# A two-layer hybrid encoder on one core: the pooling branch's GpSimd sums take a later place behind the decay chain, and a small lower-bound computation moves behind the seventh weight chunk

## The chip, the cores and the metric

The kernel runs on one core of a Trainium2 chip. The metric is device time in microseconds (us) for one execution, as the median over runs. A core has five engines with queues of their own: PE (TensorE, matrix products; its weight loads are listed as PEld), DVE (VectorE), ACT (ScalarE), POOL (GpSimd) and SP (which here issues transfers). Each engine works its queue strictly in order; an instruction whose inputs or buffers are not ready holds up everything behind it on that engine.

## The reference

The input is x with 256 tokens of 1024 features in float32. Each of two layers computes

```
x = x + 1/2 * SwiGLU_1(RMSNorm(x))
z = RMSNorm(x) @ W_in      # pool 512 | q 512 | f 512 | i 512 | out-gate 512 | branch gates 2*1024
A = causal pooling of the pool columns: 4 groups, trailing windows 2/4/8/16,
    (window mean - value) @ pool_w[g], times pool_scale
B = HGRN2 gated linear recurrence: 4 heads, 128x128 state, forget gates bounded below by lb
x = x + W_out( sigmoid(g_A) * (A @ W_pa) + sigmoid(g_B) * (B @ W_pb) )
x = x + 1/2 * SwiGLU_2(RMSNorm(x))
```

and a last RMSNorm follows. The lower bounds lb come from a softmax and a running sum over the layers' `lb_logits`, 512 numbers per layer.

## The kernel before

Weights stream in chunks of 128x2048 float32 (`stream`, `chunk`). Each chunk is split on the chip into a rounded part `hi` (ACT, L128) and a remainder `lo` (DVE, L129), and PE multiplies with both (L186 and L188, L216 to L218). There are four buffers for raw chunks and three each for `hi` and `lo`.

`mixer` (L480) holds the part that the change touches. PE first makes the f, i and q columns; then twelve steps follow (the list `steps`): two for the pool columns (`pool_in`), two for the output gate (`out_gate`, sigmoid and L673), eight for the branch gates (`gate`, L680). Each of the last ten is 24 products of 128x128 by 128x512 in L216 to L218.

Between the steps the recurrence is worked off in eight pieces, the list `recur`: seven levels, n = 1, 2, 4, 8, 16, 32, 64, and `across`. Piece i is made in step i, and its products are made in step i + 1. A level (`level`) does this:

- DVE multiplies the keys with the decays `suf` (L554) and the queries with the decays `pre` (L555) into a tile `m` of which there are two buffers.
- POOL then lengthens the decays for the next level: `suf` by L556, and `pre` by L557. L557 overwrites what L556 reads, and the next level's L554, L555 and L556 read what these two write: L556 and L557 of all levels are one chain.
- PE makes eight products from `m` (L590) in one of two PSUM tiles `gps`, and DVE takes them into the score matrix (`keep`, L565; for n = 64 ACT, L597).

The pooling branch shares POOL with that chain. `pool_group(g)` makes the running sums of group g by doubling (L636, one to four additions of about 270 columns), corrects the first 16 columns by L640 and L642, and DVE finishes the rest (L643). `pool_product(g)` multiplies the result with `pool_w` on PE (L650, L651), in one of the same two `gps` tiles, and ACT and DVE write the two parts of the product (L654, L655). All four are needed when the products with `W_pa` begin, after the twelfth step. `outputs()` (L693 on) forms the branch's output in step 9, also through `gps` tiles.

The order on each engine is laid out when the program is built: a planner with a model of durations takes, whenever an engine is free in its model, the ready instruction that stands first in the program; what is traced inside `urgent()` counts as standing 300 places earlier. The pieces of the recurrence are inside `urgent()`; the pooling calls are not. `tc.issue_after(x)` adds one rule: instructions traced in the block on x's engine are queued behind x there. Instructions of other engines in the block are not bound by it.

`lower_bounds()` (L311) runs once, in the first layer: three tiny DVE instructions (L314, L316), two exponentials on ACT (L317), and eight more tiny DVE instructions. Its result is read in the first mixer.

Of the kernel before, what the change touches and what calls it, by code (L numbers as in the profile page):

```python
# [10 lines left out]
F32 = mybir.dt.float32  # L11
# [3 lines left out]
ALU = mybir.AluOpType  # L15
# [10 lines left out]
NH = 4  # L26
# [42 lines left out]
def _body(ctx, tc, a, out):  # L69
    nc = tc.nc  # L70
# [9 lines left out]
    tt = nc.vector.tensor_tensor  # L80
# [35 lines left out]
    at = [0]  # L116
# [10 lines left out]
    def parts(raw, hi, lo, sl):  # L127
        a = nc.scalar.copy(out=hi[:, sl], in_=raw[:, sl])  # L128
        return a, tt(out=lo[:, sl], in0=raw[:, sl], in1=hi[:, sl].bitcast(F32), op=ALU.subtract)  # L129
# [14 lines left out]
    def prepare_first():  # L144


        chunks = [chunk() for _ in range(FIRST)]
        for j0, j1 in PIECES:
            sl = slice(j0 * CH // KD, j1 * CH // KD)
            c0 = 0 if j0 == 0 else NVEC + j0 * S  # L150
            xsl = slice(c0, NVEC + j1 * S)
            x = (nc.scalar if j0 == 1 else nc.sync).dma_start(out=xg[:, xsl], in_=a["x"][:, xsl])
            if j0 == 1:
                with tc.issue_after(x.ins):
                    nc.scalar.activation(table, table, AF.Silu)
            for i, (src, _, raw, hi, lo) in enumerate(chunks):
                (nc.scalar if i == j0 == 0 else nc.sync).dma_start(out=raw[:, sl], in_=src[:, sl])
                last = parts(raw, hi, lo, sl)
                if i == 0:
                    for j in range(j0, j1):  # L160
                        scaled(j, C_F1, j > 0)
        return last

    def weights(key, ahead=3):
        i = next(n for n, s in enumerate(stream) if s[0] == key)
# [79 lines left out]
    def split(out, src):  # L245

        nc.scalar.copy(out=out[0], in_=src)  # L247
        tt(out=out[1], in0=src, in1=out[0].bitcast(F32), op=ALU.subtract)  # L248

    def scaled(j, gain, first=False):  # L250

# [137 lines left out]
    def ffn(l, f, sq, gain):  # L389
        hs = slots(range(11), F32R)  # L390

        def hidden(k):
            return hs[k // 2].rearrange("p (k two) s -> p k two s", two=2)[:, k % 2]

        def gate_up(ms):
            if done:

                with tc.issue_after(done.pop().ins):
                    ws = [weights((f, l, "gu", m)) for m in ms]
            else:  # L400
                ws = [weights((f, l, "gu", m)) for m in ms]
            pss = [[pmm.tile([P, 2, S], F32, tag="mm", name="ps") for _ in range(2)] for _ in ms]
            if len(ms) == 1 and ((l, f) != (0, 0) or ms[0] > 5):

                for ks in ((range(6), range(6, KD)) if ms[0] == 0 else (range(KD),)):
                    order = [(k, g) for k in ks for g in range(2)]
                    wide_run(ws[0], [(pss[0][g], (k * 2 + g) * P, xs(k), k == 0, k == KD - 1) for k, g in order])
                return list(zip(ms, pss))
            for k0, k1 in PIECES:
                for w, ps in zip(ws, pss):  # L410
                    for kk in range(k0, k1):
                        for g in range(2):
                            c = (kk * 2 + g) * P
                            mm_wide(ps[g], w, slice(c, c + P), xs(kk), kk == 0, kk == KD - 1)
            return list(zip(ms, pss))

        def evacuate(m, pss):
            if m < 2:
                with urgent():
                    z = pair_sum(pss)  # L420
            else:
                z = pair_sum(pss)
            tt(out=z, in0=z, in1=bc(rb, 2), op=ALU.mult)  # L423
            s = tmp.tile([P, S], F32, tag="s", name="s")
            gate = nc.scalar.activation(s, z[:, 0], AF.Silu)
            h = tmp.tile([P, S], F32, tag="h", name="h")
            tt(out=h, in0=s, in1=z[:, 1], op=ALU.mult)  # L427
            split([hidden(m)[:, 0], hidden(m)[:, 1]], h)
            return gate

        n = FIRST if (l, f) == (0, 0) else 1
        groups = [range(n)] + [[m] for m in range(n, KF)]
        wait = gate_up(groups[0])
        if sq is None:
            sq = Squares()
            for j in range(KD):
                add = sq.add(j)
                if j == 1:

                    with tc.issue_after(add.ins):  # L440
                        nc.gpsimd.dma_start(out=cst, in_=a["cst"])
        with urgent():
            rc = norm_columns(sq)
        rb = None
        for ms in groups[1:]:
            wait += gate_up(ms)
            if rb is None:
                rb = norm_row(rc)
            for m, ps in wait:
                gate = evacuate(m, ps)  # L450
            wait = []
            if (f, m) == (0, 6):
                poolw = act.tile([P, NH, P], F32, tag="poolw", name="poolw")
                nc.sync.dma_start(out=poolw, in_=a["pw"][:, l])
                pw.append(poolw)
            if (l, f, m) == (0, 0, 6):
                with tc.issue_after(gate.ins), tc.issue_after(latest[1].ins):
                    lower_bounds()
                nc.sync.dma_start(out=tab, in_=a["tab"])
            if gain is None and m == 6:  # L460
                fin.extend(t.rearrange("p a b -> p (a b)") for t in slots((11, 12, 13)))
                nc.sync.dma_start(out=fin[0], in_=a["fin"])
            if gain is None and 8 <= m < 12:
                by_token(m - 8)
        if gain is None:
            return last(hidden)
        sq = Squares()
        for j in range(KD):
            ps = pmm.tile([P, 2, S], F32, tag="mm", name="ps")
            for h in range(2):  # L470
                w = weights((f, l, "dn", j, h))
                kks = [(k, h * (KF // 2) + k) for k in range(KF // 2)]
                wide_run(w, [(ps, k * P, hidden(kk), kk == 0, kk == KF - 1) for k, kk in kks])
            with urgent():
                nc.vector.scalar_tensor_tensor(
                    out=xT[:, j], in0=ps[:, 1], scalar=0.5, in1=xT[:, j], op0=ALU.mult, op1=ALU.add)
            residual(j, ps[:, 0], 0.5, gain, sq)
        return sq

    def mixer(l, sq, gain):  # L480
        big = [P, NH, S]
        kk_, pre, suf, og4 = slots((0, 2, 3, 4))
        kk_, pre, suf = (t.rearrange("p (b h) (u t) -> p b (h u) t", b=2, u=2) for t in (kk_, pre, suf))
# [54 lines left out]
        def at(t, n, first, second, one=False):  # L538


            part, (sb, _), *_ = t.ap
            return bass.AP(t.tensor, t.offset + first, [
                part, (sb + second - first, 2), (2 * n, NH * P // (2 * n)), (0 if one else 1, n)])
# [4 lines left out]
        def later(t, n):  # L548
            return at(t, n, n, 0)

        def decayed(n, left, right):

            sl, pr = earlier(suf, n), later(pre, n)
            tt(out=left, in0=earlier(kk_, n), in1=sl, op=ALU.mult)  # L554
            tt(out=right, in0=later(qx, n), in1=pr, op=ALU.mult)  # L555
            nc.gpsimd.tensor_tensor(out=sl, in0=sl, in1=at(pre, n, 2 * n - 1, 0, True), op=ALU.mult)  # L556
            nc.gpsimd.tensor_tensor(out=pr, in0=pr, in1=at(pre, n, n - 1, n, True), op=ALU.mult)  # L557

        def keep(e, n, ps):

# [86 lines left out]
        def pool_product(g):  # L647
            d = pooled[g]
            ps = pgr.tile([P, 512], F32, tag="gr", name="gps")
            mm(ps[:, 0:P], pw[l][:, g], d[:, 0:P], start=True, stop=True)  # L650
            mm(ps[:, P:S], pw[l][:, g], d[:, S - 1:P - 1:-1], start=False, stop=True, skip_group_check=True)  # L651
            sc = vec[:, C_PS + 4 * l + g:C_PS + 4 * l + g + 1]
            hl = part(phl, g)
            nc.scalar.mul(out=hl[:, 0], in_=ps[:, :S], mul=sc)  # L654
            nc.vector.scalar_tensor_tensor(  # L655
                out=hl[:, 1], in0=ps[:, :S], scalar=sc, in1=hl[:, 0].bitcast(F32), op0=ALU.mult, op1=ALU.subtract)
# [69 lines left out]
        for i, st in enumerate(steps):  # L726
            with urgent():
                if products:
                    products()
                products = recur[i]() if i < len(recur) else None  # L730
                if i == 9:
                    outputs()
            st()
            if 5 <= i < 5 + NH:
                pool_product(i - 5)
            if 3 <= i < 3 + NH:
                pool_group(i - 3)


        mg = [t.rearrange("p a b -> p (a b)") for t in slots((0, 1))]  # L740
# [33 lines left out]
                    residual(2 * i0 + j, pss[j][:, 0], 1.0, gain, sq)  # L774
        return sq

    latest = prepare_first()
    sq = None
    for l in range(L):
        sq = ffn(l, 0, sq, C_MIX + KD * l)  # L780
# [62 lines left out]
```

## Time and profile before

| what | before |
|---|---|
| median of 3 runs (lowest to highest) | 1079.44 us (1079.11 to 1079.62) |
| the profiled execution: its own time | 1079.82 us |
| its span, first to last instruction | 1078.0 us |
| mean granted TensorE clock, share of full speed | 0.998 |
| PE busy | 1064.3 us, 99% of the span |
| DVE, ACT, POOL busy | 75%, 53%, 12% |

The span is what the trace covers; the profiled execution's own time is 1.8 us longer, and that execution was 0.38 us above the median. PE's busy time counts overlapping products, so 99% busy does not mean that PE could do no better; but where PE shows no idle time, no other engine held it up.

### The profile page before, as it was taken

How to read it: one execution, taken by the hardware profiler on the slowest of the kernel's cores; microseconds unless marked ns; L12 is line 12 of the kernel's file. 1: busy time of each engine (PE TensorE's matmuls, PEld its weight loads, DVE VectorE, ACT ScalarE, POOL GpSimd, SP SyncE). 2: the span in 40 equal slices, each digit the busy share in tenths (PEclk: the TensorE clock that was granted, in tenths of full speed). 3: DMA queues.
4: the chain of work that ended last, by engine and by line, in shares of the span. 5: the costliest groups of instructions: out<-in, count | busy, mean ns of one | idle time of the engine just before them, and what ended most of it. 6: DMA issues, size and time to landing. Idle time of an engine off the chain costs nothing.

```text
span 1078.0 us, 15379 instructions
## 1 busy us (share of the span) xinstructions
PE 1064.3 (99%) x5890; PEld 918.3 (85%) x5890; DVE 813.9 (75%) x1261; ACT 566.7 (53%) x953; POOL 129.9 (12%) x130
## 2 busy tenths in 40 slices
PE   9999999999999999999999999999999999999997
PEld 7888888887888888888888888888878788888885
DVE  7887767789667987777777776777995779777642
ACT  7675544544435655554455555446345456555532
POOL 2000001038100200000100000111560011000010
PEclk9999999999999999999999999999999999999999
DMA  9755456553543655546755544674445446555441
GB/s 332 273 185 174 135 185 232 189 193 116 205 156 121 237 190 194 171 139 189 249 200 192 193 157 140 210 265 169 152 130 183 161 172 234 188 174 191 171 137 39
DMA packets 32506, 197.34 MB, mean 183 GB/s; under 512 B 3616, under 2 KB 4512, under 8 KB 14000
## 3 DMA queue, kind: packets, MB, share of 16 engines
q1 hardware_dynamic: 31824, 195.50, 52.9%
q8 instruction: 46, 0.75, 0.3%
q10 hardware_dynamic: 576, 0.79, 0.2%
q14 instruction: 28, 0.23, 0.1%
q0 software_dynamic: 32, 0.07, 0.0%
HBM read 195.29 MB, written 1.05 MB: 182 GB/s over the span
## 4 chain that ended last, share of the span: by engine, by line
PE 90%; DVE 4%; POOL 3%; issue 2%; DMA 1%; ACT 0%; POOLq 0%; SPq 0%; DVEq 0%
PE ps L186 43%; PE ps L188 22%; PE ps L218 6%; PE ps L217 6%; PE ps L216 6%; PE ps L179 4%; PE ps L180 2%; DVE lo L129 2%; POOL win L636 1%; POOL b L557 1%; POOL b L556 1%; PE gps L590 1%; DMA xg<-in_x 0%; DVE m L555 0%; PE gps L693 0%
## 5 line engine op out<-in xcount | busy, mean ns | idle before, releaser
L129 DVE TENSOR_TENSOR lo<-raw,hi 128x1024 fp32r<-128x1024 f32 (+4 forms) x406 | 461.6, 1172 | 167.8 <-ACT hi L128 128.1
L128 ACT CAST hi<-raw 128x1024 fp32r<-128x1024 f32 (+4 forms) x406 | 373.7, 967 | 276.9 <-PE ps L186 97.7
L186 PE MATMUL ps<-xs__93,hi 128*128 128x512 f32 x1504 | 363.6, 393 | 0.0
L186 PEld LDWEIGHTS ps<-xs__93,hi 128*128 128x128 f32 x1504 | 275.0, 188 | 54.1
L188 PEld LDWEIGHTS ps<-xs__93,lo 128*128 128x128 f32 x1504 | 188.7, 188 | 8.2
L188 PE MATMUL ps<-xs__93,lo 128*128 128x256 f32 x1504 | 191.1, 278 | 0.0
L186 PE MATMUL ps<-b,hi 128*128 128x512 f32 x528 | 128.7, 391 | 0.0
L186 PEld LDWEIGHTS ps<-b,hi 128*128 128x128 f32 x528 | 95.7, 188 | 17.8
L273 POOL TENSOR_TENSOR acc<-acc,sq 128x256 f32<-128x256 f32 x42 | 37.4, 890 | 606.6 <-issue 392.2
L247 ACT CAST b<-h 128x256 fp32r<-128x256 f32 x88 | 35.6, 407 | 131.1 <-DVE h L427 131.1
L217 PE MATMUL ps<-lo,xs__93 128*128 128x512 f32 x192 | 76.9, 400 | 0.0
L216 PE MATMUL ps<-hi,xs__93 128*128 128x512 f32 x192 | 76.7, 399 | 0.0
L218 PE MATMUL ps<-hi,xs__93 128*128 128x512 f32 x192 | 76.2, 397 | 0.0
L202 DVE TENSOR_TENSOR z<-ps,zl 128x256 f32<-128x256 f32 x200 | 75.2, 416 | 0.1
L188 PEld LDWEIGHTS ps<-b,lo 128*128 128x128 f32 x528 | 68.2, 188 | 4.0
L188 PE MATMUL ps<-b,lo 128*128 128x256 f32 x528 | 69.2, 278 | 0.0
L201 ACT COPY zl<-ps 128x256 f32<-128x256 f32 x200 | 63.9, 365 | 6.9 <-PE ps L188 4.2
L423 DVE TENSOR_TENSOR z<-z,rb 128x512 f32<-128x512 f32 x88 | 60.0, 685 | 0.0
L217 PE MATMUL ps<-lo,b 128*128 128x512 f32 x152 | 59.9, 394 | 0.0
L216 PE MATMUL ps<-hi,b 128*128 128x512 f32 x152 | 59.8, 397 | 0.0
L218 PE MATMUL ps<-hi,b 128*128 128x512 f32 x152 | 59.5, 396 | 0.0
L179 PE MATMUL ps<-b,hi 128*128 128x512 f32 x128 | 45.5, 398 | 0.7 <-DVE b L248 0.7
(135 smaller groups left out, 960.6 us busy)
## 6 DMA issues: line engine op xcount, KB each, us to landing
raw<-in_gu SPq DMA_DIRECT2D x82, 1024.0 KB, 4.9
raw<-in_dn SPq DMA_DIRECT2D x48, 704.0 KB, 4.1
raw<-in_wt SPq DMA_DIRECT2D x24, 1024.0 KB, 4.9
raw<-in_wi SPq DMA_DIRECT2D x12, 1024.0 KB, 4.9
raw<-in_dt SPq DMA_DIRECT2D x10, 1024.0 KB, 5.0
raw<-in_wo SPq DMA_DIRECT2D x8, 1024.0 KB, 4.9
raw<-in_gu SPq DMA_DIRECT2D x8, 512.0 KB, 8.4
raw<-in_pp SPq DMA_DIRECT2D x4, 1024.0 KB, 4.9
```

The costliest lines, as they stand in the source:

```text
L128: a = nc.scalar.copy(out=hi[:, sl], in_=raw[:, sl])
L129: return a, tt(out=lo[:, sl], in0=raw[:, sl], in1=hi[:, sl].bitcast(F32), op=ALU.subtract)
L179: mm(ps, wh[:, sl], x, start=start, stop=False)
L186: mm(ps, wh[:, c:c + P], x, start=start, stop=False)
L188: mm(ps[:, 0], wl[:, c:c + P], x[:, 0], start=False, stop=stop)
L201: nc.scalar.copy(out=zl[:, g], in_=pss[g][:, 1])
L202: tt(out=z[:, g], in0=pss[g][:, 0], in1=zl[:, g], op=ALU.add)
L216: mm(pss[h], x(k)[:, 0, th], wh[:, sl], start=k == 0, stop=False)
L217: mm(pss[h], x(k)[:, 0, th], wl[:, sl], start=False, stop=False)
L218: mm(pss[h], x(k)[:, 1, th], wh[:, sl], start=False, stop=k == nk - 1)
L273: return nc.gpsimd.tensor_add(out=self.acc, in0=self.acc, in1=sq)
L423: tt(out=z, in0=z, in1=bc(rb, 2), op=ALU.mult)
```

## The change

There are three edits.

1. `pool_group(g)` is called in step 5 + g (before: 3 + g) and `pool_product(g)` in step 7 + g (before: 5 + g).
2. Each `pool_group` stands in `tc.issue_after(marks[-1].ins)`, where `marks` collects L557 of every level. In step 5 the last mark is that of the sixth level (n = 32); in steps 6 to 8 it is that of the seventh (n = 64). So POOL's instructions of group 0 are queued behind the sixth level's decays, and those of groups 1 to 3 behind the seventh's.
3. `lower_bounds()` was bound on DVE to the end of the first two chunks' splitting; it is now bound on DVE to the last instruction of `split` for m = 6. On ACT it was and is bound to the gate of m = 6.

```
-                last = parts(raw, hi, lo, sl)
+                parts(raw, hi, lo, sl)
...
-        return last
...
     def split(out, src):
         nc.scalar.copy(out=out[0], in_=src)
-        tt(out=out[1], in0=src, in1=out[0].bitcast(F32), op=ALU.subtract)
+        return tt(out=out[1], in0=src, in1=out[0].bitcast(F32), op=ALU.subtract)
...
-            split([hidden(m)[:, 0], hidden(m)[:, 1]], h)
-            return gate
+            return gate, split([hidden(m)[:, 0], hidden(m)[:, 1]], h)
...
             if (l, f, m) == (0, 0, 6):
-                with tc.issue_after(gate.ins), tc.issue_after(latest[1].ins):
+                with tc.issue_after(gate[0].ins), tc.issue_after(gate[1].ins):
                     lower_bounds()
...
+        marks = []
+
         def decayed(n, left, right):
...
             nc.gpsimd.tensor_tensor(out=sl, in0=sl, in1=at(pre, n, 2 * n - 1, 0, True), op=ALU.mult)
-            nc.gpsimd.tensor_tensor(out=pr, in0=pr, in1=at(pre, n, n - 1, n, True), op=ALU.mult)
+            marks.append(nc.gpsimd.tensor_tensor(out=pr, in0=pr, in1=at(pre, n, n - 1, n, True), op=ALU.mult))
...
             st()
+            if 7 <= i < 7 + NH:
+                pool_product(i - 7)
             if 5 <= i < 5 + NH:
-                pool_product(i - 5)
-            if 3 <= i < 3 + NH:
-                pool_group(i - 3)
+
+                with tc.issue_after(marks[-1].ins):
+                    pool_group(i - 5)
...
-    latest = prepare_first()
+    prepare_first()
```

## Rows read from the trace of the kernel before

**Rows 1.** The page: busy time of each engine, its share of the span, instructions.

```profile
PE 1064.3 (99%) x5890; PEld 918.3 (85%) x5890; DVE 813.9 (75%) x1261; ACT 566.7 (53%) x953; POOL 129.9 (12%) x130
```

**Rows 2.** Waits on PE, whole span: line, waited for, us in total, times, longest.

```profile
PE gps L590 <- DVE m L555: 3.6, 2, 1.8
...
PE ps L179 <- DVE b L248: 0.7, 2, 0.4
...
PE gps L709 <- DVE b L248: 0.6, 2, 0.3
```

**Rows 3.** Timeline of PE around level five, first mixer: start us, duration us, instruction.

```profile
256.63 0.39 PE L218 MATMUL ps<-hi,xs__93 128*128 128x512 f32 x1
256.86 0.40 PE L216 MATMUL ps<-hi,xs__93 128*128 128x512 f32 x1
259.03 1.13 PE L590 MATMUL gps<-m 128*128 128x128 f32 x8 [1.78 <-DVE m L555]
```

**Rows 4.** Timeline of POOL in the first mixer, levels three to seven.

```profile
250.41 1.73 POOL L557 TENSOR_TENSOR b<-b 128x512 f32<-128x512 f32 x1
252.11 1.20 POOL L642 TENSOR_TENSOR pd<-pd,up 128x16 f32<-128x16 f32 x1
253.27 0.63 POOL L636 TENSOR_TENSOR win<-win 128x269 f32<-128x269 f32 x1
253.87 1.64 POOL L556 TENSOR_TENSOR b<-b,b 128x512 f32<-128x512 f32 x1
255.47 0.63 POOL L636 TENSOR_TENSOR win<-win 128x265 f32<-128x265 f32 x1
256.05 1.60 POOL L557 TENSOR_TENSOR b<-b 128x512 f32<-128x512 f32 x1
...
264.40 1.41 POOL L556 TENSOR_TENSOR b<-b,b 128x512 f32<-128x512 f32 x1 [2.49 <-DVE m L554]
265.88 1.58 POOL L557 TENSOR_TENSOR b<-b 128x512 f32<-128x512 f32 x1
267.55 1.92 POOL L556 TENSOR_TENSOR b<-b,b 128x512 f32<-128x512 f32 x1
270.17 1.91 POOL L557 TENSOR_TENSOR b<-b 128x512 f32<-128x512 f32 x1 [0.69 <-DVE m L555]
```

**Rows 5.** Timeline of DVE in the same stretch.

```profile
250.92 2.30 DVE L129 TENSOR_TENSOR lo<-raw,hi 128x1024 fp32r<-128x1024 f32 x1
...
257.69 1.20 DVE L555 TENSOR_TENSOR m<-qx,b 128x512 f32<-128x512 f32 x1 [0.38 <-POOL b L557]
```

**Rows 6.** POOL's pooling groups, 225 to 300 us: busy us, mean ns, idle before.

```profile
L636 POOL TENSOR_TENSOR win<-win 128x269 f32<-128x269 f32 (+2 forms) x6 | 4.2, 700 | 0.2
L636 POOL TENSOR_TENSOR win<-up 128x271 f32<-128x271 f32 x4 | 3.9, 976 | 0.7 <-DVE up L625 0.7
L640 POOL TENSOR_TENSOR pd<-win,tab 128x16 f32<-128x16 f32 x4 | 2.7, 686 | 0.1
L642 POOL TENSOR_TENSOR pd<-pd,up 128x16 f32<-128x16 f32 x4 | 2.3, 563 | 0.2
```

**Rows 7.** Timeline, first mixer: last pooling product, its last write, first use.

```profile
288.05 0.38 PE L650 MATMUL gps<-pd,poolw 128*128 128x128 f32 x2
...
290.44 0.48 DVE L655 SCALAR_TENSOR_TENSOR b<-gps,xg,b 128x256 fp32r<-128x256 f32 x1
...
307.25 0.39 PE L216 MATMUL ps<-hi,b 128*128 128x512 f32 x1
```

**Rows 8.** Timeline of the start and of ACT at m = 6.

```profile
16.12 0.50 PE L180 MATMUL ps<-xs__93,lo 128*128 128x256 f32 x2 [0.69 <-DVE lo L129]
...
16.77 0.23 DVE L316 TENSOR_TENSOR sm<-xg,sm 128x4 f32<-128x4 f32 x2
16.97 1.23 DVE L129 TENSOR_TENSOR lo<-raw,hi 128x1024 fp32r<-128x1024 f32 x1
...
53.59 1.28 ACT L317 ACT_TABLE_LOAD   x1
```

## Prediction

> **What bounds the kernel now.** I read the page first. PE is busy for 1064.3 of 1078.0 us and no other engine comes near [rows 1]. So a change to POOL or DVE can give back only time in which PE stands still, and the next view is the list of waits on PE. Between the first and the last products it is short. The largest entry is L590, the products of a level, waiting for L555, the DVE instruction that finishes the level's second factor: 3.6 us, twice, once in each mixer. The others are two small waits at the end of each mixer, 0.7 and 0.6 us in all [rows 2]. The reader should see that one place carries nearly all of the time that an edit in the mixers could win.
>
> The timeline of PE shows that place. Products of L216 to L218 start 0.23 us apart (256.63 to 256.86), so the next instruction was due at 256.86 + 0.23 = 257.09. It is L590 of the fifth level, n = 16, and it starts at 259.03 [rows 3]. The stall is 1.94 us; the view writes 1.78 because it lets the earlier product end later. Both mixers: 2 x 1.94 = 3.88 us.
>
> Then I ask what made L555 late. It waited for POOL's L557 of the fourth level: the releaser stands in its row, 0.38 us [rows 5]. In the timeline of POOL, L557 of the third level ends at 250.41 + 1.73 = 252.14. Its successor in the chain, L556 of the fourth level, starts at 253.87, which is 1.73 us later, and in between POOL did two instructions of the pooling branch (L642, L636). L556 ends at 253.87 + 1.64 = 255.51; L557 follows at 256.05, 0.54 us later, with another L636 in between [rows 4]. So 1.73 + 0.54 = 2.27 us of the chain that ended at the stall were sums of the pooling branch, which nobody needs until much later.
>
> **The change part by part.** *The sums are queued behind the decays.* Nothing is removed or added: in each mixer the ten L636, four L640 and four L642 come to 4.2 + 3.9 + 2.7 + 2.3 = 13.1 us of POOL [rows 6], before and after. They move from among levels two to five to behind level six (group 0) and seven (groups 1 to 3). On the chain the fourth level loses 2.27 us of foreign work. The stall is 1.94 us, so at an unchanged order of PE it disappears with 0.33 us to spare. I take -1.94 us for each mixer: -3.88 us.
>
> What stands behind the sums now? On POOL only the reciprocal root of `outputs()` and the next chunk of norm work. In the trace before, the chain ends at 270.17 + 1.91 = 272.08 [rows 4]; 13.1 us more is 285.2 even if all of the sums came after it.
>
> *The products of the branch two steps later.* The last pooling product ran at 288.05 and its last write ended at 290.44 + 0.48 = 290.92. Two steps of 24 products at 0.23 us are 11 us, so the product comes at about 299 and the write ends at about 302. The first product with `W_pa` starts at 307.25, and its fourth block of weights, the first that reads group 3, is nine products later, at 309.3 [rows 3, 7]. I cost the move at nothing: 7 us of gate products cover it. Were that cover gone, PE would wait one for one, and twice.
>
> *DVE and ACT.* L643, L654 and L655 move with their groups out of a crowded stretch into an easier one; they are off the chain of PE. I take nothing, and no less than nothing.
>
> *The lower bounds.* L314 and L316 leave the start: the two L316 took 0.23 us, so all three about 0.35 us by estimate, ahead of an L129. PE's last wait there, 0.69 us, ended at 16.12, before they ran [rows 8], so no wait of PE is behind them: 0, with -0.35 us as the bound on the good side. At m = 6 the two exponentials now stand behind three DVE instructions that stand behind `split`. On ACT, whatever is queued after them (copies out of PSUM, casts) waits with them, some 0.35 us, under weights that are prepared three chunks ahead. The dear mishap is an activation between the two exponentials: each change of table loads for 1.28 us [rows 8], twice, 2.56 us of ACT at a stage where PE waits for nothing; 0 as long as chunks are ahead, 2.56 us at the very worst. The edits move no transfer: the loads of `tab` and `pool_w` stay where they are on SP's queue.
>
> *A rule to weigh.* Beside DVE's work POOL is slow, and DVE is slow beside POOL's: L642, 16 columns wide, took 1.20 us where its group's mean is 0.56, while an L129 of DVE took 2.30 us, against 1.23 in the start [rows 4 to 6, 8]. The Trainium skill (SBUF — State Buffer, "Who interferes with whom") says that a DVE instruction with two inputs in SBUF and a GpSimd instruction that reads SBUF exclude one another, and that the second to start is held until the first is done. It speaks against the change: the decays themselves read SBUF beside L129, L554 and L555, so taking the sums away leaves them exposed. By the rows alone the sum is 1075.6; by the rule at its full strength it would be the second rival's.
>
> **The sum.** 1079.82 (the profiled execution's own time: 1078.0 of span and 1.8 around it) - 3.88 = 1075.94. That execution was 0.38 us above the median of 1079.44, so on the median's scale 1075.56.
>
> **The rivals.** *The stall moves (same).* The order on PE is planned anew. The sums also stood in the planner's chain; without them it believes each level ready sooner and puts the products earlier. PE then meets the next level too early by about as much as it did. For this: the fifth level's place on PE was already a planner's guess that was 1.94 us too early, and 0.33 us to spare is thin. Against it: the three foreign instructions in the chain ran late on the chip, and what made the guess wrong goes with them. The time is that of before, 1079.4; a stall of half the size gives 1077.5, still under the bound of 0.2%.
>
> *The bare chain is slower than planned (slower).* Place: L590 of levels four to seven. With POOL to itself, a level costs L556 + L557. Where DVE was quiet they took 1.41 + 1.58 = 2.99 us, beside DVE's splitting 1.92 + 1.91 = 3.83 us [rows 4]. If the plan has the quiet pace and the chip runs at the other, each of four levels is 0.84 us late on PE, 3.4 us for a mixer in place of 1.94: 1079.44 + 2 x (3.36 - 1.94) = 1082.3. It decides against the change once a level is more than 1.94 / 4 = 0.49 us behind its plan. For it: DVE was never idle for long around the stall, and now more level work falls into fewer microseconds. Against it: a chain that is done early can only be late if the plan follows it closely, and the other engines' buffers (two tiles `m`, two `gps`) set a slower pace than POOL in levels six and seven, where L556 waited 2.49 us for DVE [rows 4].
>
> *The pooled products arrive late (slower).* L693 and the pooling products share two PSUM tiles, and both now fall into the tenth and eleventh steps. Against it stands the margin of 7 us; if it is lost and 1 us more, 1079.4 - 3.9 + 2 = 1077.5, and only beyond 3.9 us does it turn the sign. That is unlikely.
>
> **How the numbers follow.** A measurement of this kernel tells some 0.2% (2.2 us) from no change: below 1077.3 is faster, above 1081.6 slower. Forecast, the stall goes: 0.52. The stall moves: 0.26. The bare chain: 0.18. Late pooled products or a mishap of the tables that outweighs the gain: 0.04. So faster 0.52, same 0.26, slower 0.22. The likeliest case's own range is 1074.2 to 1077.2: downwards the two small waits at the end of a mixer could go too, 0.7 + 0.6 = 1.3 us in all [rows 2]; upwards a stall of 0.8 us may remain in each mixer. The whole range must take in no change and the nearer half of the bare chain's case: 1074.2 to 1081.6.
>
> **What would show it.** If I am right, POOL's timeline has L556 and L557 of levels two to six with no L636, L640 or L642 in between, the sums as a block behind them, and L590's entry among PE's waits has shrunk from 3.6 us to under 1 us; the last L655 still ends before the first product with `W_pa`. If the stall moved, the entry stays, at another level. If the bare chain is the bound, there are several waits of L590 for L554 or L555 in a mixer, each with POOL as what released DVE. For the lower bounds, L314 appears after 53 us and not in the start, with one load of the table for L317 and one back. The prediction is wrong above all if the newly planned order of PE leans on the shortened chain harder than the old one did.

## Result, and the profile after

The changed kernel takes 1090.1 us (median of 4 runs, 1089.63 to 1091.09), the kernel before beside it 1079.45 (4 runs, 1079.11 to 1079.62). The ratio is 1.0100, with a 95% interval of 1.0088 to 1.0112: 1% slower. The forecast was 1075.6 with a range up to 1081.6. The profiled span is 1088.2 us, 10.2 more than before's 1078.0.

The line of busy times on the profile's page of the changed kernel, which answers to [rows 1], has every engine within 2.8 us of its old work:

```profile
PE 1066.6 (98%) x5890; PEld 921.1 (85%) x5890; DVE 814.7 (75%) x1261; ACT 567.5 (52%) x953; POOL 131.7 (12%) x130
```

So PE stands still for longer. The view of waits on PE of the changed kernel (line, waited for, us in total, times, longest) answers to [rows 2]:

```profile
PE ps L178 <- DVE b L247: 10.4, 2, 5.2
PE gps L590 <- DVE m L555: 1.2, 2, 0.6
```

(The `lo` and `hi` products and `split` stand one line higher here: L178, L179 and L247 are L179, L180 and L248 of [rows 2]. The merges at the end of `mixer` stand two lines lower: L753, L759, L760 were L751, L757, L758.) The stall that the change was costed on fell from 3.6 to 1.2 us, and the two small waits at the end of a mixer, 0.7 and 0.6, are not in the list any more. A new wait of 5.2 us has appeared at the end of each mixer.

**Where the gain came from.** The timeline of POOL in the first mixer of the changed kernel, to be held against [rows 4]:

```profile
253.06 1.17 POOL L557 TENSOR_TENSOR b<-b 128x512 f32<-128x512 f32 x1 [1.83 <-DVE m L555]
254.99 1.43 POOL L556 TENSOR_TENSOR b<-b,b 128x512 f32<-128x512 f32 x1 [0.76 <-DVE m L554]
...
260.96 1.40 POOL L556 TENSOR_TENSOR b<-b,b 128x512 f32<-128x512 f32 x1 [2.49 <-DVE m L554]
...
263.99 0.63 POOL L636 TENSOR_TENSOR win<-up 128x271 f32<-128x271 f32 x1
...
281.96 1.08 POOL L642 TENSOR_TENSOR pd<-pd,up 128x16 f32<-128x16 f32 x1
```

No sum stands among the decays until 263.99; after it the sums run as one block but for the seventh level's two decays, and the last ends at 283.04. Between the decays POOL now mostly waits for DVE. The seventh level is the exception: its L555 on DVE still waits for POOL's L557 of the sixth level, and PE's products wait for that L555. The timelines of DVE and PE:

```profile
264.06 1.11 DVE L555 TENSOR_TENSOR m<-qx,b 128x512 f32<-128x512 f32 x1 [0.96 <-POOL b L557]
```

```profile
265.32 1.13 PE L590 MATMUL gps<-m 128*128 128x128 f32 x8 [0.59 <-DVE m L555]
```

The sixth level's decays ran at the pace that the prediction called quiet (1.40 us here for L556 at 260.96, 1.58 us for L557 at 262.44), but they started late, after a wait of 2.49 us for DVE.

**Where the loss came from.** The timeline of PE in the first mixer of the changed kernel, only the products that take a `gps` tile after the levels, and the first product with `W_pa` (305.73):

```profile
278.42 0.38 PE L650 MATMUL gps<-pd,poolw 128*128 128x128 f32 x2
...
286.30 0.38 PE L650 MATMUL gps<-pd,poolw 128*128 128x128 f32 x2
...
287.20 1.05 PE L693 MATMUL gps<-vt,at__2287 128*128 128x128 f32 x8
...
297.44 0.60 PE L709 MATMUL gps<-cst,b 128*128 128x128 f32 x4
...
305.73 0.39 PE L215 MATMUL ps<-hi,b 128*128 128x512 f32 x1
...
309.93 0.60 PE L709 MATMUL gps<-cst,b 128*128 128x128 f32 x4
310.37 0.39 PE L650 MATMUL gps<-pd,poolw 128*128 128x128 f32 x2
...
316.19 0.39 PE L650 MATMUL gps<-pd,poolw 128*128 128x128 f32 x2
```

Before, the four pooling products stood at 266.07, 273.01, 281.57 and 288.05, the last of them [rows 7] just ahead of `outputs()`. Now the first two run before `outputs()` and the last two only after all of it: L693 and its turning L709 for one half of the branch, then for the other. All of these take the two `gps` tiles, and in this trace, as in every other one here, they take them in the order of the program: step 9 makes `outputs()` before it makes product 2. Group 2's product stands behind the L709 at 309.93, though its sums were done by 283.

What follows is seen on DVE. The timeline of DVE at the end of the first mixer of the changed kernel: L655 is the last writing of a pooling product, L759 and L753 merge the products with `W_hp` and `W_pa`, L760 adds them, L247 prepares the sum for the last products:

```profile
312.42 0.69 DVE L759 TENSOR_TENSOR z<-ps,b 128x512 f32<-128x512 f32 x1 [0.15 <-PE ps L217]
...
317.35 0.48 DVE L655 SCALAR_TENSOR_TENSOR b<-gps,xg,b 128x256 fp32r<-128x256 f32 x1 [3.18 <-ACT b L654]
318.94 0.69 DVE L759 TENSOR_TENSOR z<-ps,b 128x512 f32<-128x512 f32 x1 [1.11 <-PE ps L217]
...
322.67 1.88 DVE L753 TENSOR_TENSOR b<-ps,b 128x512 f32<-128x512 f32 x3 [0.24 <-PE ps L217]
...
325.07 0.68 DVE L753 TENSOR_TENSOR b<-ps,b 128x512 f32<-128x512 f32 x1
325.67 1.22 DVE L129 TENSOR_TENSOR lo<-raw,hi 128x1024 fp32r<-128x1024 f32 x1
...
327.40 3.49 DVE L129 TENSOR_TENSOR lo<-raw,hi 128x1024 fp32r<-128x1024 f32 x3
330.81 1.29 DVE L759 TENSOR_TENSOR z<-ps,b 128x512 f32<-128x512 f32 x2
332.01 2.36 DVE L129 TENSOR_TENSOR lo<-raw,hi 128x1024 fp32r<-128x1024 f32 x2
334.27 0.42 DVE L247 TENSOR_TENSOR b<-gps,b 128x256 fp32r<-128x256 f32 x1
```

In the kernel before, the four merges with `W_pa` were spread out (310.25, 313.54, 320.48, 325.75), each ahead of its partner with `W_hp`. Here two of the L759 come first, since PE has `W_hp`'s products ready while the last two pooled groups are missing (the products with `W_pa` start on the groups that are there), and all four L753 fall into 3 us, at 322.67 to 325.75. The adding, the turning and L247 come behind them and behind six weight remainders (L129, six of them from 325.67 on, 7.07 us). Then the timeline of PE shows the price:

```profile
329.47 1.04 PE L709 MATMUL gps<-cst,z 128*128 128x128 f32 x8
335.69 0.80 PE L178 MATMUL ps<-b,hi 128*128 128x512 f32 x1 [5.18 <-DVE b L247]
...
336.49 0.63 PE L178 MATMUL ps<-b,hi 128*128 128x512 f32 x1
...
337.13 0.63 PE L178 MATMUL ps<-b,hi 128*128 128x512 f32 x1
```

In the kernel before, the first of these products started 4.2 us earlier (timeline of PE):

```profile
331.48 0.50 PE L179 MATMUL ps<-b,hi 128*128 128x512 f32 x1 [0.36 <-DVE b L248]
```

The pairs of L178 and L179 that follow are 0.64 us apart (336.49 to 337.13); before, the same pairs were 0.35 us apart (331.94 to 332.29). The view by stretches of the changed kernel says why (stretch, its length, busy us and instructions of PE, PEld, DVE, ACT and POOL, PE's granted clock, DMA share, GB/s):

```profile
330.50:335.60 5.10, 0.01 (x1) 0.00 (x0) 5.10 (x9) 2.08 (x5) 0.00 (x0) 0.96 1.06 398
335.60:338.40 2.80, 2.71 (x8) 2.33 (x9) 1.30 (x4) 0.37 (x1) 0.00 (x0) 0.50 0.85 336
338.40:341.00 2.60, 2.60 (x18) 2.35 (x17) 0.00 (x0) 0.00 (x0) 0.00 (x0) 0.95 0.05 19
...
870.40:874.00 3.60, 3.51 (x11) 3.02 (x12) 1.30 (x4) 0.37 (x1) 0.00 (x0) 0.50 0.99 412
```

After the wait PE ran at 0.50 of its clock for 2.8 us in the first mixer and 3.6 us in the second; at half speed half of that is lost, an estimate of 1.4 + 1.8 = 3.2 us.

The sum of the trace: L590 -2.4 us, the two small waits -1.3, the new wait +10.4, the clock behind it +3.2, and +0.5 because the first transfer of x landed 0.49 us later in this execution (DVE's first instruction on it, L255, starts at 4.37 us; it started at 3.88). Together +10.4, against +10.2 in the span.

### The profile page after: what moved, and what is told of

It is laid out like the page before. It is cut to its first block, busy times and chain, and to the rows that moved or that the text cites. A ratio compares the mean times of both kernels' runs of the same rounds, so it can differ in the third digit from the quotient of the medians.

```text
span 1088.2 us, 15391 instructions
## 1 busy us (share of the span) xinstructions
PE 1066.6 (98%) x5890; PEld 921.1 (85%) x5890; DVE 814.7 (75%) x1261; ACT 567.5 (52%) x953; POOL 131.7 (12%) x130
## 4 chain that ended last, share of the span: by engine, by line
PE 93%; DVE 4%; issue 1%; DMA 1%; POOL 1%; ACT 0%; POOLq 0%; SPq 0%; DVEq 0%
PE ps L185 43%; PE ps L187 22%; PE ps L215 6%; PE ps L216 6%; PE ps L217 6%; PE ps L178 4%; PE ps L179 2%; DVE lo L129 2%; PE gps L590 1%; DMA xg<-in_x 0%; DMA raw<-in_gu 0%; DVE m L555 0%; PE gps L693 0%; PE gps L574 0%; PE gps L709 0%
## 5 line engine op out<-in xcount | busy, mean ns | idle before, releaser
L129 DVE TENSOR_TENSOR lo<-raw,hi 128x1024 fp32r<-128x1024 f32 (+4 forms) x406 | 463.3, 1179 | 159.4 <-ACT hi L128 119.1
L185 PE MATMUL ps<-b,hi 128*128 128x512 f32 x528 | 128.7, 391 | 0.0
L178 PE MATMUL ps<-b,hi 128*128 128x512 f32 x128 | 48.7, 419 | 10.4 <-DVE b L247 10.4
```

What stands on the lines that cost most here:

```text
L178: mm(ps, wh[:, sl], x, start=start, stop=False)
L185: mm(ps, wh[:, c:c + P], x, start=start, stop=False)
```

## Experiments

The theory at this point: the loss is made by the order in which the two `gps` tiles are handed out, so the last two pooled products wait behind `outputs()`. The rivals: lateness of the products itself; the queueing of the sums; the lower bounds. In the expectations "the second run" is the one with the products in another PSUM tile, and "the third run" the one with the products late and nothing else.

**The products in the same step as their sums.** The changed kernel with each product called right behind its sums, in step 5 + g, so that `outputs()` asks for its tiles last again. That is the step that the products had before, so this is the queueing of the sums without the move of the products.

```
-            if 7 <= i < 7 + NH:
-                pool_product(i - 7)
             if 5 <= i < 5 + NH:
                 with tc.issue_after(marks[-1].ins):
                     pool_group(i - 5)
+                pool_product(i - 5)
```

> The changed kernel, but pool_product(g) is called right behind pool_group(g) in step 5 + g, so that all four products stand ahead of outputs() in the program. Queue theory (products of groups 2 and 3 wait because the two gps tiles are handed out in program order and outputs() asks for four of them first): the last L650 runs before the first L693, near 288 us; the wait of L178 for L247 at the end of a mixer falls from 5.2 us to below 1 us; the gain of the early part stays; 1075.5 us (1074 to 1077.5). Rival, late sums (the sums themselves end at 282 us, 9 us later than before, and that is what makes the end of the mixer late): the sums end as late as in the changed kernel, so 1088 to 1091 us.

Measured: 1079.74 us (10 runs, 1079.13 to 1080.55), ratio to before 1.0001, interval 0.9992 to 1.0010. The waits on PE of this kernel:

```profile
PE gps L650 <- POOL pd L642: 2.6, 2, 1.3
...
PE ps L178 <- DVE b L247: 0.7, 2, 0.4
```

The time is not the expected 1075.5, because the early gain did not stay. But the 5.2 us waits are gone, with all of the loss: the last product runs at 289.18, ahead of L693 at 289.40. L590 is not in the list any more, but product 0 now meets its late sums (1.27 us at 269.65), and the small wait at the end is that of before. Of the 3.6 us that the queueing gave, 2.6 went to L650; the other 1.0 shows as 0.3 us in the span (1077.7) and as nothing in the median. So the loss hangs on where the products stand; this run doesn't tell yet whether by the queue for the tiles or by their lateness.

**The products in another PSUM tile.** The changed kernel, products where the change put them, but in the gate products' tile. No product is earlier in the program than in the changed kernel.

```
-            ps = pgr.tile([P, 512], F32, tag="gr", name="gps")
+            ps = pmm.tile([P, 512], F32, tag="mm", name="ps")
```

> The changed kernel with steps 5 and 7 as they are, but pool_product takes its PSUM tile from the five of the token products instead of the two gps tiles. Queue theory: the products of groups 2 and 3 no longer stand behind the four tiles of outputs(); they run near 294 and 301 us in place of 310 and 316, in time for the products with W_pa, and the wait of L178 falls below 1.5 us: 1074.5 to 1078 us. Rival, late position (two steps later is too late whatever tile they use) or late sums: 1087 to 1091 us.

Measured: 1076.35 us (6 runs, 1075.87 to 1076.95), ratio 0.9970, interval 0.9959 to 0.9981: 13.75 us below the changed kernel, and 3.2 below the kernel before (1079.6 in the same runs). Its waits on PE, and under them its timeline of PE in the first mixer:

```profile
PE gps L590 <- DVE m L555: 1.2, 2, 0.6
...
PE gps L609 <- DVE m L604: 0.8, 2, 0.4
```

```profile
272.24 1.06 PE L693 MATMUL gps<-vt,at__2287 128*128 128x128 f32 x8
...
300.93 0.38 PE L650 MATMUL ps<-pd,poolw 128*128 128x128 f32 x2
```

L693 doesn't stand between the products any more; it comes 15 us earlier than in the changed kernel. The last product is at 300.93, where the prediction had put it (about 299).

**The same, one step later still.** The kernel of the run before with the products in step 8 + g.

```
-            if 7 <= i < 7 + NH:
-                pool_product(i - 7)
+            if 8 <= i < 8 + NH:
+                pool_product(i - 8)
```

> The changed kernel with the branch's products in the gate products' PSUM tile (as in the run that was fastest, 1076.35 us), and each product one step later still. If only the queue for the two shared PSUM tiles was the loss, lateness without that queue is harmless until the last product comes so late that the last merges wait for it: the last product would move from 300.9 to some 306 to 312 us, still ahead of the across products' end, and the time would be 1076.3 to 1079 us, with no wait of 5 us of L178. If lateness itself was the loss, and the tile only a side matter, the wait of L178 of 5 us in each mixer comes back, and the time is about 1087 to 1090 us.

Measured: 1076.41 us (6 runs, 1076.15 to 1076.50), ratio 0.9971, interval 0.9959 to 0.9982. The timeline of PE of this kernel, the last pooled product and the first with `W_pa`:

```profile
306.69 0.38 PE L650 MATMUL ps<-pd,poolw 128*128 128x128 f32 x2
...
307.05 0.48 PE L215 MATMUL ps<-hi,b 128*128 128x512 f32 x1
```

All four products are later than in the run before, the last by 5.8 us and only 0.36 us ahead of the first use of `W_pa`, and the time is the same within 0.1 us. Lateness up to that point costs nothing. What cost was the queue for the two tiles, which pushed the last two products beyond that point. Whether products as late as 310 and 316 us would cost the same without the queue, no run shows.

**The products late, nothing else.** The kernel before with its products in step 7 + g, and one more buffer for the sums, which now live longer.

```
-            d = tmp.tile([P, S], F32, tag="pd", name="pd", bufs=3)
+            d = tmp.tile([P, S], F32, tag="pd", name="pd", bufs=4)
...
-            if 5 <= i < 5 + NH:
-                pool_product(i - 5)
+            if 7 <= i < 7 + NH:
+                pool_product(i - 7)
```

> The kernel before with one edit: pool_product(g) in step 7 + g instead of 5 + g (and a fourth buffer for its input, without which the calls could not stand in that order); the sums stay where they were, with nothing queued behind the decays. Queue theory: the products of groups 2 and 3 fall behind outputs() as in the changed kernel, so the loss at the end of each mixer is there without the gain in the early part: 1079.4 + 2 x 6.6 = 1092 us (1087 to 1094). Rival, late sums: the sums are as early as before, so 1079.4 us (1078 to 1081).

Measured: 1100.58 us (4 runs, 1100.13 to 1102.59), ratio 1.0198, interval 1.0184 to 1.0212. Its waits on PE:

```profile
PE ps L179 <- DVE b L248: 10.4, 2, 5.2
PE gps L590 <- DVE m L555: 9.3, 6, 2.4
```

The wait at the end is the same as in the changed kernel to the tenth (products 2 and 3 at 313.82 and 319.64). What I hadn't expected is the second row: with the products out of their way, PE waits for the levels' L555 three times in a mixer (1.77, 0.52 and 2.38 us) instead of once. So the late products alone cost 21 us. In the profiled execution, with 20.9 us more of span, the waits are 5.7 + 10.4 - 1.3 = 14.8 us of it; by estimate most of the rest is half clock, 6.7 us: 4.2 and 5.7 us at 0.50 behind the waits at the end of the two mixers, and 3.5 us at 0.51 behind the wait of 2.38 us in the second mixer.

**The change without its queueing.**

```
-                with tc.issue_after(marks[-1].ins):
-                    pool_group(i - 5)
+                pool_group(i - 5)
```

> The changed kernel without issue_after around pool_group: the same steps, 5 and 7, the sums free to run whenever POOL is idle in the plan. Queue theory: the end of each mixer loses as much as in the changed kernel; the early part gets the sums between the decays again and, as in the third run, with levels no longer slowed by pooled products in their PSUM queue, two or three waits of L590 in a mixer: 1095 to 1101 us. Rival, the step alone holds the sums back and the queueing adds nothing: 1089 to 1091 us.

Measured: 1099.47 us (4 runs, 1098.47 to 1100.58), ratio 1.0185, interval 1.0169 to 1.0200. L590 waits 8.7 us in 6 times, L178 10.4 in 2. Queueing the sums is thus worth 1099.47 - 1090.1 = 9.4 us inside the change: it is the good part, though beside products that were not moved (the first experiment) it was worth nothing.

**The other PSUM tile alone.** The kernel before with the one-line edit of the tile.

> The kernel before with one edit: pool_product takes its PSUM tile from the five of the token products; the sums stay among the decays. If the queueing of the sums is what makes the second run fast: the levels are planned sooner, as in the third run, and PE waits two or three times for L555 in each mixer; 1079.4 + 2 x (4.6 - 1.9) = 1085 us (1081 to 1087). Rival, the free PSUM tiles alone are the gain and the queueing adds nothing: 1076 to 1077 us.

Measured: 1083.27 us (5 runs, 1082.99 to 1084.86), ratio 1.0037, interval 1.0024 to 1.0050. The timeline of PE, levels of the first mixer:

```profile
258.90 1.13 PE L590 MATMUL gps<-m 128*128 128x128 f32 x8 [1.77 <-DVE m L555]
264.87 1.13 PE L590 MATMUL gps<-m 128*128 128x128 f32 x8 [0.17 <-DVE m L555]
270.01 1.13 PE L590 MATMUL gps<-m 128*128 128x128 f32 x8 [2.39 <-DVE m L555]
```

These are nearly the waits of the two kernels told just before. What the three have in common is that no pooled product takes a `gps` tile before the last level's products; the products of the fifth to the seventh level then stand within 11.1 us (258.90 to 270.01), where the kernel before has 17.4 us for them (259.03 [rows 3] to 276.48). DVE makes their inputs no later than before (the seventh level's L555 starts at 268.32, before at 268.48); it is PE that comes sooner. Only the fifth level's L555 waited for POOL (0.38 us, as in [rows 5]). The seventh level's stands right behind a weight remainder, as the timeline of DVE shows:

```profile
266.30 2.10 DVE L129 TENSOR_TENSOR lo<-raw,hi 128x1024 fp32r<-128x1024 f32 x1
268.32 1.54 DVE L555 TENSOR_TENSOR m<-qx,b 128x512 f32<-128x512 f32 x1
```

In the changed kernel that L555 starts at 264.06, ahead of the next L129 (265.09). So at the seventh level the gain of the queueing came with a new order on DVE, and not from a wait for POOL that it took away. The tile alone is +3.6 us, with the change -3.2.

**The products one step later.** The changed kernel with the products in step 6 + g, between the first experiment and the change.

```
-            if 7 <= i < 7 + NH:
-                pool_product(i - 7)
+            if 6 <= i < 6 + NH:
+                pool_product(i - 6)
```

> The changed kernel with pool_product(g) in step 6 + g: only group 3 now stands behind outputs() in the program, not groups 2 and 3. Queue theory: one late product is enough, since every column block of the products with W_pa reads all four groups; group 3 comes near 310 us and the wait at the end of a mixer stays, perhaps smaller: 1083 to 1090 us. Rival, a matter of amount (two late products cost twice as much as one): about half of the loss, 1083 to 1085 us. If the last product comes before outputs() anyway, 1076 to 1080 us, and the place in the program decides less than I think.

Measured: 1084.4 us (4 runs, 1083.33 to 1084.83), ratio 1.0043, interval 1.0028 to 1.0058. The time fits the expectation and its rival alike; the place is in neither. Only product 3 comes after `outputs()`, at 313.55, and no wait of L178 follows. The timeline of PE shows another one, at the products of `across`:

```profile
281.58 1.74 PE L609 MATMUL gps<-m 128*128 128x128 f32 x8 [2.81 <-DVE b L655]
```

L609 waits for a `gps` tile that a pooled product holds until L655 has read it: the same queue, another victim, 2 x 2.8 us. Two products behind `outputs()` bring the wait at the end, one doesn't.

**All sums behind the seventh level.** The kernel of the other PSUM tile with `pool_group(i - 6)` from step 6 on.

> The second run (products in a PSUM tile of their own) with pool_group(g) in step 6 + g, so that all four groups are queued behind the seventh level's decays. In the second run a sum and a correction of group 0 stand between the sixth and the seventh level's decays, and PE waits 0.6 us for the seventh level and 0.4 us for the last products, in each mixer. If those sums cause these waits: 1074.4 us (1073.5 to 1075.6). Rival, the waits are DVE's and stay: 1076.3 us (1075.8 to 1077); group 3 could also come late, 1077 us or more.

Measured: 1077.17 us (9 runs, 1076.38 to 1077.57), ratio 0.9976, interval 0.9966 to 0.9986. L590 is down to 0.3 us, but L609 waits for L604 2 x 1.24 us instead of 2 x 0.4. The wait moved by one stage, and nothing is won; the expected 1074.4 was missed.

**All one step earlier.** The kernel of the other PSUM tile with `pool_group(i - 4)` from step 4 and `pool_product(i - 6)` from step 6 on.

> The same kernel with the fastest run's PSUM tile, the pooling sums queued one step earlier (from the fifth step on) and the products one step earlier. If the decays of the early levels are still ahead of the sums, the waits on POOL's decays stay at 1.2 us or below and the time is 1075.5 to 1077 us. If the sums of the first group get in front of the decays of the sixth level again, L590 waits 1 to 2 us more in each mixer and the time is 1078 to 1080 us.

Measured: 1076.81 us (11 runs, 1076.12 to 1077.74), ratio 0.9976, interval 0.9967 to 0.9985. L590 waits 2 x 0.96 us, level seven alone. Within the spread of the two better runs; the version with only the other PSUM tile stays the best found.

**The lower bounds alone.** The kernel before with the third edit only.

> The kernel before with the third edit alone: lower_bounds() behind split for m = 6. By the prediction's sum 0: 1079.4 us (1078.9 to 1079.9), the three small instructions gone from the start. Rival, the start is disturbed: the changed kernel's trace runs 0.54 us behind from its first products on; if the third edit does that, 1080.0 us or more.

Measured: 1079.54 us (11 runs, 1078.82 to 1080.07), ratio 1.0000, interval 0.9991 to 1.0009, with the waits of [rows 2] in it. The edit costs nothing that these runs could tell (the interval is about 1 us to either side), and the late start in the trace after isn't its doing: here L255 starts at 3.90 us.

## Why the prediction was wrong

**The sums queued behind the decays: right in kind, too large.** The stall at the fifth level is gone, as forecast, and the sums are a block that ends at 283.04 (bound given: 285.2). But a wait of 0.59 us at the seventh level took its place (0.77 by the starts on PE, as the prediction had measured its 1.94), within the 0.8 us that the text allowed: the term was about 1.2 us for each mixer, not 1.94. The first product with `W_pa` starts 1.5 us earlier than before in spite of the late start, 2.0 us with it taken off; that looks like the forecast 1.94 and isn't, because two pooled products, 0.37 us each (310.37 to 310.74), now stand behind that point. With the products in another PSUM tile, where nothing is put off, -3.2 us is measured in place of -3.88, and the waits give -2.9 of it: -2.4 at L590, -1.3 at the end of the mixers, +0.8 at L609.

**The step that failed: "I cost the move at nothing: 7 us of gate products cover it".** The sum "two steps of 24 products at 0.23 us are 11 us, so the product comes at about 299" holds if a moved product meets nothing on its way. It met `outputs()`, made in step 9 and inside `urgent()`, which asks for the same two tiles ahead of groups 2 and 3. Products 2 and 3 ran at 310.37 and 316.19, the last L655 at 317.35 and not at 302. With a tile of their own the same calls gave 300.93, the forecast place, and no loss. The margin of 7 us was there too: the run one step later still used up nearly all of it, without cost.

**The rival that had the place.** *The pooled products arrive late* named L693 and the two shared tiles, and got 0.04. It weighed them against a margin in time, though the tiles were taken as a queue in the order of the program: moved past step 9, product 2 did not start before `outputs()` was through (three kernels), however early its sums were. It also priced the lateness as a wait one for one where the products with `W_pa` begin. PE didn't wait there; it did the products with `W_hp` first. The price came 25 us later, at the last products, when DVE had merges, weight remainders and L247 all to do: 5.2 us, and 1.4 to 1.8 us of half clock behind it.

**The other rivals.** *The stall moves* came true in a small way (0.59 us at the seventh level; L609 where all sums stand behind the seventh). *The bare chain* named several waits in a mixer with POOL as what released DVE; there was one, that of 0.59 us, behind decays at the quiet pace. Elsewhere POOL's decays, 1.04 to 2.45 us each in the first mixer, held up no products. The three waits of L590 with the sums still among the decays were in no case of the forecast. **The lower bounds** at 0 agree with their run. **DVE and ACT**, costed at nothing, did the same work by the busy line, but the place of that work was not free: the 5.2 us wait is a wait for DVE. The rule weighed from the Trainium skill (SBUF — State Buffer, "Who interferes with whom") didn't bring the second rival about: the decays beside DVE's work left 0.59 us of wait. No run here tested the rule itself.

**What is read and not tested.** That the merges of all four `W_pa` results in 3 us on DVE make the 5.2 us wait is read from the timeline; no run moved a merge alone. Tested is that it comes with two pooled products behind `outputs()` (the change, the late products alone, the change without queueing) and is absent in all the others, where at most one product takes a `gps` tile behind `outputs()`. That the levels' products close up because the pooled ones left their tiles, and that the queueing helps the seventh level by the order on DVE, is also read from traces; the planner's order was not changed by itself.

## What to carry to other kernels

Before a step is moved by some iterations, list what else asks for its buffers between the old and the new place: here the tiles of a pool were taken in program order, so a move past another user was a move behind all of that user's chain, whatever the margin in time. Where two edits are made together, run each alone: here the queueing alone was worth nothing, the move alone cost 21 us, both together cost 10.6, and one line that gave the products another tile turned +10.6 us into -3.2. The parts do not add up; the traces show another order on PE and DVE after each edit. And follow a late result to its last reader: PE filled the gap with other products and paid 25 us later.

## What the runs showed of the hardware

The clock after a stall. When PE had waited 5.18 us at the end of a mixer, the next 2.8 us (first mixer) and 3.6 us (second) ran at a granted clock of 0.50, that is at the lower of the two levels, and then it came back. In the kernel of the products one step later, a wait of 2.81 us was followed by 3.5 us at a mean of 0.51, and the second mixer's wait of 2.84 us likewise. The length of a wait did not decide alone. A wait of 2.38 or 2.39 us for the seventh level stands in three kernels, once in each mixer. In that of the other PSUM tile alone the clock behind both was 1.00. In that of the late products alone it was 1.00 behind the first and 0.51 for 3.5 us behind the second, in the change without its queueing the other way round. The view by stretches, behind the waits of 2.81 us (products one step later), 2.38 us (no queueing, first mixer) and 2.39 us (the other tile alone, first mixer):

```profile
281.90:285.40 3.50, 3.50 (x14) 3.02 (x13) 2.20 (x3) 0.59 (x1) 0.00 (x0) 0.51 0.99 330
...
270.80:274.30 3.50, 3.50 (x13) 2.92 (x12) 3.50 (x6) 0.74 (x2) 1.42 (x1) 0.51 0.60 169
...
270.00:273.00 3.00, 2.99 (x18) 2.69 (x19) 3.00 (x5) 1.21 (x4) 2.91 (x3) 1.00 0.33 57
```

Behind the waits of 1.78 us in the kernel before (259.0 to 261.8 us in the first mixer) the clock was 1.00. The Trainium skill (TensorE: Matmul & The Clock Gate, "Part 1: The HAM clock gate") says that the gate has just two states, 1.2 and 2.4 GHz, and falls back after idling; the trace agrees, with 0.50 and 1.00. The prediction had no clock in the price of any rival; behind the new wait the clock added an estimated 3.2 us to 10.4.
